# Where h tiles and down weights begin in SBUF, modulo 256 bytes, in a two-layer decoder kernel

## The chip, the cores and the metric

The kernel runs on one core of one Trainium2 chip. The metric is the device time of one execution in microseconds (us); lower is better.

## What is computed

Two layers (DEPTH = 2), each of three sub-layers: a SwiGLU feed-forward net (FFN), a token mixer with three kinds of attention heads, and a second FFN. The input has 256 tokens of width 1024, in float32. Cut to what matters here:

```python
def swiglu(h, w_gate, w_up, w_down):
    return (jax.nn.silu(h @ w_gate) * (h @ w_up)) @ w_down        # D_FF = 2816

for layer in range(DEPTH):
    g = norm_gains[layer]
    h = rmsnorm(x, g[0])
    x = x + 0.5 * rmsnorm(swiglu(h, w_ffn_gate[layer, 0], w_ffn_up[layer, 0], w_ffn_down[layer, 0]), g[1])
    h = rmsnorm(x, g[2])
    x = x + rmsnorm(token_mixer(h, w_in[layer], w_out[layer], ...), g[3])
    h = rmsnorm(x, g[4])
    x = x + 0.5 * rmsnorm(swiglu(h, w_ffn_gate[layer, 1], w_ffn_up[layer, 1], w_ffn_down[layer, 1]), g[5])
```

## The kernel before

**Split products.** Each float32 matrix is split into a high part (rounded to fp32r, by ScalarE) and a low part (the difference, by VectorE), and `mm3` (which calls `mm`, line 385) makes three matmuls of each product: high by high, high by low, low by high. Weights land in `raw` tiles by DMA and are split into a `ring` of ten tiles (ScalarE line 294, VectorE line 297).

**The FFN.** The 2816 hidden columns are handled as 11 pairs j of 256 (two chunks c of 128). In `gb(j)` the weights of gate and up are the stationary operand and the activations `xt` move, 256 columns a matmul, 96 matmuls a pair; line 605 is silu, line 607 the product, and lines 608 and 609 write its high and low parts to two `h` tiles of 512 columns: columns 256c + 128T belong to chunk c and token half T. In `down(j, T)` an h block of 128 columns is stationary and a row of 512 down weights moves, 12 matmuls: first the six of chunk 0, then the six of chunk 1 (each of two output halves n, three matmuls each). The first pair or two of an FFN go by `ga` and `hturn` in its place: there `xt` is stationary, and the product is transposed into the h tiles (lines 576, 582, 583).

**Order.** The loop runs `gb(j)`, `down(j - 1, 0)`, `down(j - 1, 1)`. For the pairs 6 to 10 (the set `skip`) `down(j, 1)` is put off; it comes at the end of the FFN by `LAST_ORDER = ((9, 0), (6, 1), (10, 0), (7, 1), (8, 1), (9, 1), (10, 1))`. So for the pairs 0 to 5 the two downs stand one behind the other, in each of the four FFNs: 24 such double downs. A list scheduler (`Program.run`) with a table of assumed durations decides the order on each engine.

**Places.** Tiles of the pools `xt`, `h2` and `ring` begin at a place: `AT_... = n` stands for 64 n bytes past a multiple of 256 bytes, by padding inside the tile (`PLACE` = 16 floats = 64 bytes, `Slots.take`). Blocks of 128 float32 columns are 512 bytes, so all blocks of a tile have their tile's place. `xt` has place 0. Gate, up and the other weights have place 1 (`AT_W`, `AT_X`), the h tiles place 1 (`AT_H`), the mixer's output weights and its own h tiles place 1 (`AT_O`), and the down weights have place 1 for chunk 0 and place 0 for chunk 1 (`AT_D = (1, 0)`). In this text the **distance** of a matmul is the place of the stationary block that is loaded for the next matmul less the place of the data that it streams itself, in bytes modulo 256. Before, chunk 0 of every down has distance 0, chunk 1 has 64, and `gb` has 64.

**Norms.** A norm takes the sum of squares with two ScalarE instructions (`sumsq`, line 428) whose squares go into `junk` tiles that nobody reads; then come GpSimd (lines 437, 438) and VectorE (457 for the residual, 476 for the normed rows), the transposes on TensorE (505), and the split into `xt` (508, 511). `junk` has two buffers, used in turn.

Of the kernel before, what the change touches and what calls it, by code (L numbers as in the profile page):

```python
# [8 lines left out]
F32 = mybir.dt.float32  # L9
F32R = mybir.dt.float32r  # L10
BF16 = mybir.dt.bfloat16
AF = mybir.ActivationFunctionType
OP = mybir.AluOpType
# [22 lines left out]
LAST_ORDER = ((9, 0), (6, 1), (10, 0), (7, 1), (8, 1), (9, 1), (10, 1))  # L36
# [31 lines left out]

BASE_PAD = 32
PLACE = 16  # L70
AT_W, AT_X, AT_O = 1, 1, 1
AT_H, AT_D = 1, (1, 0)


class Slots:
# [17 lines left out]
    def take(self, dtype, place=0):  # L93
        i = self.idle.pop(0)
        self.n += 1
        if self.places:
            u = self.whole(i, dtype)
            o = PLACE * ((place - i * (self.places - 1)) % 4)
            w = self.shape[1]
            t = [u[:, o + w * p:o + w * (p + 1)] for p in range(self.parts)]  # L100
        else:
            t = [self.pool.tile(self.shape, dtype, tag=f"{self.tag}{i}_{p}", name=f"{self.tag}{i}_{p}_{self.n}") for p in range(self.parts)]
        return i, (t[0] if self.parts == 1 else t)
# [17 lines left out]
class Program:  # L121
# [7 lines left out]
    def op(self, eng, dur, fn, after=(), bufs=(), spare=None, lag=None):  # L129
        o = Op()  # L130
        o.eng, o.dur, o.fn, o.after, o.bufs = eng, dur, fn, [a for a in after if a is not None], list(bufs)
        o.spare, o.lag, o.idx = spare or {}, lag, len(self.ops)
        for b in o.bufs:
            b.left += 1
        self.ops.append(o)
        return o
# [99 lines left out]
def act_us(n, psum, extra=0):  # L236
    return (0.05 if psum else 0.092) + 0.000833 * n + 0.093 * extra


def dve_us(n):  # L240
    return 0.068 + 0.00104 * n


def trunk(tc, x, norm_gains, w_gate, w_up, w_down, w_in, w_out, dlam, subln, consts, out):
    nc = tc.nc
    ctx = ExitStack()
    P1 = ctx.enter_context(tc.tile_pool(name="one", bufs=1))
# [4 lines left out]
    op = G.op  # L252
    PS = Slots(PSM, "ps", 8, [128, 512])
    P1.tile([128, BASE_PAD], F32, name="basepad")
    XTS = Slots(P1, "xt", 1, [128, KC * SEQ], 2, 1)
    H2 = Slots(P1, "h2", 12, [128, 512], 1, 4)
    RNG = Slots(P1, "ring", RING, [128, 1024], 2, 4)
    RAW = Slots(P1, "raw", NRAW, [128, 1024])
    ES = Slots(P1, "e", N_ES, [128, 512])
# [3 lines left out]
    SM = Slots(P1, "sm", 24, [128, 4])  # L263
    GPO = Slots(P1, "gpo", 1, [128, D])
    GPR = Slots(P1, "gpr", 1, [128, D])
    JK = Slots(P1, "junk", 2, [128, 512])
    QB = tuple(slice(32 * m, 32 * (m + 1)) for m in range(4))
    HB = (slice(0, 64), slice(64, 128))
    HALF = (slice(0, 512), slice(512, 1024))
# [1 line left out]
    def TS(T):  # L271
        return slice(128 * T, 128 * (T + 1))
# [42 lines left out]
    def half_row(w, r0, place):  # L315
        return half([(lambda t: t, w[r0:r0 + 128, :])], CUT_R, place)
# [44 lines left out]
    def warm():  # L361

        z, p = Buf(H2, BF16), Buf(PS)
        o = op("POOL", 0.2, lambda: nc.gpsimd.memset(z.t, 0.0), [], [z])

        def more(n, us, after):
            def pe():
                for _ in range(n):
                    mm(p.t, z.t[:, 0:128], z.t, True, True)

            op("PE", us, pe, [o, *after], [z, p])

        return more
# [10 lines left out]
    def mm(o, a, b, start=False, stop=False):  # L384
        nc.tensor.matmul(o, a, b, start=start, stop=stop, skip_group_check=True)  # L385
# [152 lines left out]
    def ffn(l, s, xt, na, turn1, g, final, nxt, pre):  # L538

        wg, wu, wd = w_gate[l, s], w_up[l, s], w_down[l, s]  # L540
        tiles = dict(pre)

        def tile_(kind, j):
            if (kind, j) not in tiles:
                if kind == "D":
                    tiles[kind, j] = [half_row(wd, 256 * j + 128 * c, AT_D[c]) for c in range(2)]
                else:
                    tiles[kind, j] = half_cols(wg if kind == "G" else wu, 256 * j, AT_X if j < na else AT_W)
            return tiles[kind, j]
# [3 lines left out]
        def hbuf(j):  # L553
            if j not in hb:
                hb[j] = (Buf(H2, F32R, AT_H), Buf(H2, F32R, AT_H))
            return hb[j]

        hdone = {}
        rows = {}
# [9 lines left out]
        def hturn(j, T):  # L569
            sg, m = rows[j, T]  # L570
            p = Buf(PS)
            bh, bl = hbuf(j)

            def pe():
                for c in range(2):
                    nc.tensor.transpose(p.t[:, 128 * c:128 * (c + 1)], sg.t[:, 256 + 128 * c:256 + 128 * (c + 1)], ident)  # L576

            def view(t):
                return t.rearrange("p (m t) -> p m t", m=2)

            o = op("PE", 0.22, pe, [m, o_ident], [p, sg])
            o1 = op("ACT", act_us(256, True), lambda: nc.scalar.activation(view(bh.t)[:, :, TS(T)], view(p.t[:, :256]), AF.Copy), [o], [p, bh])
            o2 = op("DVE", dve_us(256), lambda: nc.vector.tensor_tensor(view(bl.t)[:, :, TS(T)], view(p.t[:, :256]), view(bh.t)[:, :, TS(T)].bitcast(F32), OP.subtract),
                    [o1], [p, bh, bl])
            hdone[j, T] = [o2]

        def gb(j):
            sg = Buf(ES)
            a = None
            bh, bl = hbuf(j)  # L590
            for part in range(2):
                p = Buf(PS)
                hs = tile_("GU"[part], j)
                os = []
                for m in range(2):
                    for ks in steps(STEPS_G):
                        def pe(m=m, p=p, hs=hs, ks=ks):
                            for k in ks:
                                wh, wl = wk(hs, k)
                                c = TS(m)  # L600
                                mm3(p.t[:, 256 * m:256 * (m + 1)], wh[:, c], wl[:, c], xt.hi(k, slice(0, 256)), xt.lo(k, slice(0, 256)), m == 0 and k == 0, k == KC - 1)
                        use = [hs[i] for i in sorted({k // 4 for k in ks})]
                        os.append(op("PE", 0.327 * len(ks), pe, os[-1:] + sum(xt.done, []) + sum((h.ready for h in use), []), [p, xt.b] + [h.ring for h in use]))
                if part == 0:
                    a = op("ACT", act_us(512, True), lambda p=p: nc.scalar.activation(sg.t, p.t, AF.Silu), os[-1:], [p, sg])  # L605
                else:
                    m_ = op("DVE", dve_us(512), lambda p=p: nc.vector.tensor_tensor(sg.t, p.t, sg.t, OP.mult), os[-1:] + [a], [p, sg])  # L607
                    o1 = op("ACT", act_us(512, False), lambda: nc.scalar.activation(bh.t, sg.t, AF.Copy), [m_], [sg, bh])  # L608
                    o2 = op("DVE", dve_us(512), lambda: nc.vector.tensor_tensor(bl.t, sg.t, bh.t.bitcast(F32), OP.subtract), [o1], [sg, bh, bl])  # L609
                    hdone[j, 0] = hdone[j, 1] = [o2]  # L610

        acc = [Buf(PS) for _ in range(4)]
# [2 lines left out]
        def down(j, T):  # L615
            bh, bl = hbuf(j)
            last = j == NPAIR_FF - 1
            hs = tile_("D", j)
            for pieces in ([[(0, 0), (1, 0)], [(0, 1), (1, 1)]] if last else [[(0, 0), (0, 1)], [(1, 0), (1, 1)]]):
                cs = sorted({c for c, _ in pieces})  # L620
                ns = sorted({n for _, n in pieces})

                def pe(pieces=pieces):
                    for c, n in pieces:
                        o = slice(256 * c + 128 * T, 256 * c + 128 * (T + 1))
                        w = hs[c].ring.t
                        mm3(acc[2 * T + n].t, bh.t[:, o], bl.t[:, o], w[0][:, HALF[n]], w[1][:, HALF[n]], j == 0 and c == 0, last and c == 1)

                o = op("PE", 1.30, pe, hdone[j, T] + sum((done[2 * T + n] for n in range(2)), []) + sum((hs[c].ready for c in cs), []),
                       [acc[2 * T + n] for n in ns] + [bh, bl] + [hs[c].ring for c in cs])  # L630
                for n in (ns if last else range(2)):
                    done[2 * T + n] = [o]
# [13 lines left out]
        else:  # L646
# [1 line left out]
            hturn(0, 0)  # L648
            ga(0, 1)
            hturn(0, 1)  # L650
        skip = {j for j, T in LAST_ORDER if T == 1}
        for j in range(na, NPAIR_FF):
            gb(j)
            if j == NPAIR_FF - 1:
# [14 lines left out]
    def mixer(l, xt, turn1, g, nxt, o_cst, o_misc):  # L669
# [5 lines left out]
        def vstep(T, t):  # L675
            if vt[t] is None:
                vt[t] = half_v(wi, t)
            if t % 2 == 0:
                V[T, t // 2] = (Buf(PS), Buf(H2), [])
            p, v, os = V[T, t // 2]  # L680
            os.append(rows_op(p, 256 * (t % 2), xt, T, vt[t], t % 2 == 0))
            if t % 2 == 1:
                if t // 2:
                    o = op("ACT", act_us(512, True), lambda: nc.scalar.activation(v.t, p.t, AF.Copy), os, [p, v])
                else:
                    o = op("DVE", dve_us(512), lambda: nc.vector.tensor_copy(v.t, p.t), os, [p, v])
                vdone[T, t // 2] = o

        tab = [None]
# [247 lines left out]
        n = len(PAIRS)  # L937
# [162 lines left out]
```

## Time and profile before

| | |
|---|---|
| Three runs | 1002.55, 1003.51, 1003.85 us; median 1003.51 us |
| The profiled execution's own time | 1003.59 us |
| Its span, first to last instruction | 1001.8 us; so 1.8 us lie around it |
| TensorE matmuls (PE) busy | 986.3 us, 98% of the span |
| TensorE weight loads (PEld) busy | 909.8 us, 91% |
| VectorE (DVE), ScalarE (ACT), GpSimd (POOL) busy | 63%, 58%, 3% |
| Granted TensorE clock, mean | 0.999 of full speed |

Busy time of a matmul includes the part in which it overlaps the next, so a busy share near 100% says that TensorE has next to no idle time, not that its matmuls follow at the best rate. The rate is read from the distance between starts. The weight load of the next matmul starts within a few ns of the start of a matmul, so the starts of the PEld rows give it.

### The profile page before, as it was taken

The page shows a single profiled execution, that of the slowest core. Times are in us where ns is not written, and L with a number is a line of the kernel's source. Part 1 is how long each engine was busy: PE and PEld are TensorE (multiplying, and loading weights), DVE is VectorE, ACT ScalarE, POOL GpSimd, SP SyncE. Part 2 cuts the span into 40 slices and gives each one's busy share as a digit, 9 for nine tenths or more (in the row PEclk, how much of TensorE's full clock was granted, in tenths as well). Part 3 has the DMA queues.
Part 4 walks back from the last instruction along what each step waited for, and adds up shares of the span by engine and source line. Part 5 has one row for each costly group of instructions (what it writes and reads, how often), then busy time and mean ns, then how long its engine had stood idle before and what let it go on. Part 6 is the DMA issues. An engine that isn't in the chain of part 4 may idle for free.

```text
span 1001.8 us, 18113 instructions
## 1 busy us (share of the span) xinstructions
PE 986.3 (98%) x7144; PEld 909.8 (91%) x7144; DVE 632.5 (63%) x1123; ACT 582.8 (58%) x1133; POOL 34.3 (3%) x59
## 2 busy tenths in 40 slices
PE   8999999999999999999999999999999999999997
PEld 6999999898888999999899999999998789999995
DVE  6755544778898655444685554458799776545433
ACT  7654443769996545444665444446899765544441
POOL 1000000100001000000000000002000020000000
PEclk9999999999999999999999999999999999999999
DMA  8986664683335766665577666557732457666531
GB/s 265 335 271 192 189 184 147 196 252 106 109 116 177 248 185 190 197 188 151 171 227 233 194 191 199 152 169 237 204 106 85 155 161 233 188 195 187 167 105 43
DMA packets 157432, 182.86 MB, mean 183 GB/s; under 512 B 6049, under 2 KB 141473, under 8 KB 157218
## 3 DMA queue, kind: packets, MB, share of 16 engines
q1 hardware_dynamic: 157202, 181.43, 59.6%
q8 instruction: 56, 0.92, 0.4%
q14 instruction: 30, 0.25, 0.1%
q10 hardware_dynamic: 144, 0.26, 0.1%
HBM read 180.62 MB, written 1.05 MB: 181 GB/s over the span
## 4 chain that ended last, share of the span: by engine, by line
PE 87%; ACT 8%; DVE 2%; issue 1%; POOL 1%; DMA 0%; DVEq 0%; POOLq 0%; SPq 0%; ACTq 0%
PE ps L385 86%; ACT q L722 2%; ACT ring L294 1%; ACT q L738 1%; PE ps L505 1%; ACT e L789 1%; ACT junk L428 0%; DVE q L726 0%; ACT sn L867 0%; ACT sn L868 0%; DMA grow<-in_norm_gains 0%; ACT sn L866 0%; DVE q L742 0%; POOL sm L438 0%; PE ps L576 0%
## 5 line engine op out<-in xcount | busy, mean ns | idle before, releaser
L294 ACT ACTIVATE ring<-raw 128x512 fp32r<-128x512 f32 (+1 forms) x552 | 368.0, 706 | 319.8 <-issue 228.9
L297 DVE TENSOR_TENSOR ring<-raw,ring 128x512 fp32r<-128x512 f32 (+1 forms) x552 | 414.7, 788 | 198.4 <-ACT ring L294 192.5
L385 PE MATMUL ps<-xt,ring 128*128 128x256 f32 x4320 | 505.9, 277 | 0.0
L385 PEld LDWEIGHTS ps<-xt,ring 128*128 128x128 f32 x4320 | 499.9, 188 | 5.2 <-issue 1.7
L385 PE MATMUL ps<-ring,h 128*128 128x512 f32 x1248 | 299.7, 394 | 0.0
L385 PEld LDWEIGHTS ps<-ring,h 128*128 128x128 f32 x1248 | 229.6, 188 | 49.5 <-issue 0.3
L385 PE MATMUL ps<-ring,xt 128*128 128x256 f32 x1056 | 129.8, 281 | 1.5 <-DVE xt L511 1.5
L385 PEld LDWEIGHTS ps<-ring,xt 128*128 128x128 f32 x1056 | 126.5, 188 | 2.8 <-DVE xt L511 2.1
L607 DVE TENSOR_TENSOR e<-ps,e 128x512 f32<-128x512 f32 x37 | 25.6, 692 | 102.7 <-PE ps L385 102.7
L437 POOL TENSOR_SCALAR sm<-sm 128x1 f32<-128x1 f32 x24 | 15.8, 660 | 917.6 <-ACT junk L428 704.5
L608 ACT ACTIVATE h<-e 128x512 fp32r<-128x512 f32 x37 | 23.2, 626 | 21.3 <-DVE e L607 21.3
L453 DVE TENSOR_TENSOR e<-ps,gpo 128x512 f32<-128x512 f32 x24 | 16.4, 688 | 21.7 <-ACT junk L428 21.5
L428 ACT ACTIVATE junk<-ps 128x512 bf16<-128x512 f32 x24 | 14.3, 596 | 26.7 <-PE ps L385 25.6
L385 PE MATMUL ps<-q,q 128*128 128x256 f32 (+3 forms) x128 | 25.9, 295 | 3.1 <-DVE q L727 2.1
L738 ACT ACTIVATE q<-ps 64x256 fp32r<-64x256 f32 x72 | 27.1, 377 | 0.8
L385 PEld LDWEIGHTS ps<-q,q 128*128 128x128 f32 (+1 forms) x128 | 19.4, 187 | 8.5 <-issue 1.6
L605 ACT ACTIVATE e<-ps 128x512 f32<-128x512 f32 x37 | 21.9, 593 | 5.9 <-PE ps L385 5.8
L609 DVE TENSOR_TENSOR h<-e,h 128x512 fp32r<-128x512 f32 x37 | 25.3, 684 | 0.0
L789 ACT ACTIVATE e<-sn,sm 128x256 f32<-128x256 f32 (+1 forms) x56 | 24.7, 446 | 0.1
L722 ACT ACTIVATE q<-ps 32x256 fp32r<-32x256 f32 x64 | 24.0, 375 | 0.9
L742 DVE SCALAR_TENSOR_TENSOR q<-ps,q 64x256 fp32r<-64x256 f32 x48 | 20.2, 421 | 1.0
L508 ACT ACTIVATE xt<-ps 128x512 fp32r<-128x512 f32 x24 | 13.3, 591 | 11.5 <-PE ps L505 11.4
(86 smaller groups left out, 397.1 us busy)
## 6 DMA issues: line engine op xcount, KB each, us to landing
raw<-in_w_ffn_gate SPq DMA_DIRECT2D x88, 512.0 KB, 4.6
raw<-in_w_ffn_up SPq DMA_DIRECT2D x88, 512.0 KB, 4.7
raw<-in_w_ffn_down SPq DMA_DIRECT2D x88, 512.0 KB, 4.4
raw<-in_w_in SPq DMA_DIRECT2D x40, 512.0 KB, 5.3
raw<-in_w_out SPq DMA_DIRECT2D x16, 512.0 KB, 3.6
raw<-in_w_in SPq DMA_DIRECT2D x16, 256.0 KB, 4.2
gpo<-in_norm_gains SPq DMA_DIRECT2D x6, 512.0 KB, 5.8
gpr<-in_norm_gains SPq DMA_DIRECT2D x5, 512.0 KB, 5.1
```

The source lines that it names most:

```text
L294: nc.scalar.activation(h.ring.t[0][:, s], raw.t[:, s], AF.Copy)
L297: nc.vector.tensor_tensor(h.ring.t[1][:, s], raw.t[:, s], h.ring.t[0][:, s].bitcast(F32), OP.subtract)
L385: nc.tensor.matmul(o, a, b, start=start, stop=stop, skip_group_check=True)
L453: nc.vector.tensor_tensor(y.t, accs[i].t, gv(), OP.mult)
L605: a = op("ACT", act_us(512, True), lambda p=p: nc.scalar.activation(sg.t, p.t, AF.Silu), os[-1:], [p, sg])
L607: m_ = op("DVE", dve_us(512), lambda p=p: nc.vector.tensor_tensor(sg.t, p.t, sg.t, OP.mult), os[-1:] + [a], [p, sg])
L608: o1 = op("ACT", act_us(512, False), lambda: nc.scalar.activation(bh.t, sg.t, AF.Copy), [m_], [sg, bh])
L609: o2 = op("DVE", dve_us(512), lambda: nc.vector.tensor_tensor(bl.t, sg.t, bh.t.bitcast(F32), OP.subtract), [o1], [sg, bh, bl])
L722: nc.scalar.activation(b.t[QB[e], :], p.t[QB[m], :256], AF.Copy, scale=scale)
L738: nc.scalar.activation(bs[b].t[HB[b ^ e], :], p.t[HB[b], :256], AF.Copy, scale=scale)
L742: nc.vector.scalar_tensor_tensor(lo[b].t[HB[b ^ other], :], p.t[HB[b], :256], scale, bs[b].t[HB[b], :].bitcast(F32), OP.mult, OP.subtract)
L789: nc.scalar.activation(e.t[:, SEG[a]], sn.t[:, SEG[a]], AF.Exp, bias=mn.t[:, a:a + 1], scale=-1.0, accum_out=den.t[:, d0 + a:d0 + a + 1])
```

## The change

Down weights, h tiles and the mixer's output weights and h tiles all get place 0, the place of `xt`. The h tiles get 16 floats more, and from a cut on their columns lie 64 bytes further: for the pairs 6 to 10 all of chunk 1 (cut at 256), for the others the block of chunk 1 and token half 1 alone (cut at 384), which is the block that a double down reads last. Instructions that write h tiles are split at the cut, since no single run of columns crosses it. `junk` loses one of its two buffers.

```diff
-AT_W, AT_X, AT_O = 1, 1, 1
-AT_H, AT_D = 1, (1, 0)
+AT_W, AT_X, AT_O = 1, 1, 0
+AT_H, AT_D = 0, 0
...
-            o = PLACE * ((place - i * (self.places - 1)) % 4)
+            cols = self.parts * self.shape[1] + PLACE * (self.places - 1)
+            o = PLACE * ((place - i * (cols // PLACE)) % 4)
...
-    H2 = Slots(P1, "h2", 12, [128, 512], 1, 4)
+    H2 = Slots(P1, "h2", 12, [128, 512 + PLACE], 1, 4)
...
-    JK = Slots(P1, "junk", 2, [128, 512])
+    JK = Slots(P1, "junk", 1, [128, 512])
...
-                    tiles[kind, j] = [half_row(wd, 256 * j + 128 * c, AT_D[c]) for c in range(2)]
+                    tiles[kind, j] = [half_row(wd, 256 * j + 128 * c, AT_D) for c in range(2)]
...
+        skip = {j for j, T in LAST_ORDER if T == 1}
+
+        def hcut(j):
+
+            return 256 if j in skip else 384
+
+        def hcol(j, c, T):
+            o = 256 * c + 128 * T
+            o += PLACE if o >= hcut(j) else 0
+            return slice(o, o + 128)
+
+        def hparts(j):
+            n = hcut(j)
+            return (slice(0, n), slice(0, n)), (slice(n, 512), slice(n + PLACE, 512 + PLACE))
...
-            o1 = op("ACT", act_us(256, True), lambda: nc.scalar.activation(view(bh.t)[:, :, TS(T)], view(p.t[:, :256]), AF.Copy), [o], [p, bh])
...
+            o1 = op("ACT", 2 * act_us(128, True), fhi, [o], [p, bh])
+            o2 = op("DVE", 2 * dve_us(128), flo, [o1], [p, bh, bl])
...
-                    o1 = op("ACT", act_us(512, False), lambda: nc.scalar.activation(bh.t, sg.t, AF.Copy), [m_], [sg, bh])
-                    o2 = op("DVE", dve_us(512), lambda: nc.vector.tensor_tensor(bl.t, sg.t, bh.t.bitcast(F32), OP.subtract), [o1], [sg, bh, bl])
+
+                    def fhi():
+                        for f, t in hparts(j):
+                            nc.scalar.activation(bh.t[:, t], sg.t[:, f], AF.Copy)
+
+                    def flo():
+                        for f, t in hparts(j):
+                            nc.vector.tensor_tensor(bl.t[:, t], sg.t[:, f], bh.t[:, t].bitcast(F32), OP.subtract)
+
+                    o1 = op("ACT", act_us(256, False) * 2, fhi, [m_], [sg, bh])
+                    o2 = op("DVE", dve_us(256) * 2, flo, [o1], [sg, bh, bl])
...
-                        o = slice(256 * c + 128 * T, 256 * c + 128 * (T + 1))
+                        o = hcol(j, c, T)
```

On TensorE nothing moves. These are the rows of `down(1, 0)`, chunk 1, and `down(1, 1)`, chunk 0, in the first FFN, before (the h tiles with the lower number hold the high part, the others the low part):

```order
L385 MATMUL ps_0_16_508<-ring_16_503,h_4_532 128x512 x2
L385 MATMUL ps_0_16_508<-ring_16_503,h_5_546 128x512
L385 MATMUL ps_0_17_509<-ring_16_503,h_4_532 128x512 x2
L385 MATMUL ps_0_17_509<-ring_16_503,h_5_546 128x512
L385 MATMUL ps_0_18_538<-ring_15_474,h_4_532 128x512 x2
L385 MATMUL ps_0_18_538<-ring_15_474,h_5_546 128x512
L385 MATMUL ps_0_19_539<-ring_15_474,h_4_532 128x512 x2
L385 MATMUL ps_0_19_539<-ring_15_474,h_5_546 128x512
```

The changed kernel has the same eight rows in the same place, and so for all of TensorE; the names' last numbers and the line differ, and the addresses, which these rows don't print. On ScalarE, the instruction that writes the high part of h in `gb(3)` of the first FFN, with its neighbours, before and now:

```order
L294 ACTIVATE ring_28_838<-raw_0_28_726 128x1024
L294 ACTIVATE ring_29_875<-raw_0_29_737 128x512 x2
L608 ACTIVATE h_8_880<-e_0_5_835 128x512
L294 ACTIVATE ring_30_889<-raw_0_30_772 128x512 x2
...
L295 ACTIVATE ring_28_846<-raw_0_28_733 128x1024
L295 ACTIVATE ring_29_883<-raw_0_29_745 128x512 x2
L632 ACTIVATE h_8_888<-e_0_5_843 128x384
L632 ACTIVATE h_8_888<-e_0_5_843 128x128
L295 ACTIVATE ring_30_898<-raw_0_30_780 128x512 x2
```

One instruction has become two in its place; the same holds for VectorE behind it. In all, ScalarE and VectorE have 51 instructions more each (37 of `gb`, 14 of `hturn`). Last, ScalarE where the first layer's mixer ends: the squares of token half 0 of the mixer's output (from ps) and of the new x (from xs), before and now. The number right behind junk is the buffer:

```order
L428 ACTIVATE junk0_0_13_3708,sm22_0_47_3707<-ps6_0_91_3497 128x512
L428 ACTIVATE junk1_0_14_3718,sm22_0_47_3707<-ps2_0_92_3498 128x512
...
L428 ACTIVATE junk0_0_15_3745,sm23_0_49_3744<-xs_87 128x512
L428 ACTIVATE junk1_0_16_3748,sm23_0_49_3744<-xs_87 128x512
...
L429 ACTIVATE junk0_0_13_3732,sm22_0_47_3731<-ps6_0_91_3521 128x512
L429 ACTIVATE junk0_0_14_3742,sm22_0_47_3731<-ps2_0_92_3522 128x512
...
L429 ACTIVATE junk0_0_15_3769,sm23_0_49_3768<-xs_87 128x512
L429 ACTIVATE junk0_0_16_3772,sm23_0_49_3768<-xs_87 128x512
```

The order is the same, but each square now waits on ScalarE's own semaphore for the end of the square just before it, where it waited for the one before that. On SyncE and GpSimd nothing moves.

## Rows read from the trace of the kernel before

**Rows 1.** The page: span, TensorE's busy time, and the chain by engine.

```profile
span 1001.8 us, 18113 instructions
...
PE 986.3 (98%) x7144; PEld 909.8 (91%) x7144; DVE 632.5 (63%) x1123; ACT 582.8 (58%) x1133; POOL 34.3 (3%) x59
...
PE 87%; ACT 8%; DVE 2%; issue 1%; POOL 1%; DMA 0%; DVEq 0%; POOLq 0%; SPq 0%; ACTq 0%
```

**Rows 2.** The chain in order of time: one stretch of the first FFN.

```profile
29.23 164.53 PE ps L385 x1188
```

**Rows 3.** Timeline of weight loads, double down of pair 0 (start, us, what).

```profile
37.25 1.56 PEld L385 LDWEIGHTS ps<-ring,h 128*128 128x128 f32 x7
...
38.63 1.59 PEld L385 LDWEIGHTS ps<-ring,h 128*128 128x128 f32 x7
...
40.03 1.57 PEld L385 LDWEIGHTS ps<-ring,h 128*128 128x128 f32 x7
...
41.41 1.12 PEld L385 LDWEIGHTS ps<-ring,h 128*128 128x128 f32 x5
```

**Rows 4.** Timeline of weight loads: the first mixer's output product, places all 1.

```profile
308.51 8.35 PEld L385 LDWEIGHTS ps<-ring,h 128*128 128x128 f32 x37
```

**Rows 5.** Weight loads of gb: behind that down, 1.2 us later, and another gb.

```profile
42.81 0.88 PEld L385 LDWEIGHTS ps<-xt,ring 128*128 128x128 f32 x7
...
44.07 1.55 PEld L385 LDWEIGHTS ps<-xt,ring 128*128 128x128 f32 x13
...
26.02 1.60 PEld L385 LDWEIGHTS ps<-xt,ring 128*128 128x128 f32 x13
```

**Rows 6.** Weight loads of down(0, 0), chunk 0, second FFN, behind ga.

```profile
344.25 1.10 PEld L385 LDWEIGHTS ps<-ring,h 128*128 128x128 f32 x5
```

**Rows 7.** Timeline of ScalarE in the first mixer.

```profile
244.03 0.53 ACT L867 ACTIVATE sn<-sn 128x384 f32<-128x384 f32 x1
244.59 0.53 ACT L868 ACTIVATE sn<-sn 128x384 f32<-128x384 f32 x1
245.02 0.47 ACT L866 ACTIVATE sn<-ps 128x384 f32<-128x384 f32 x1
```

**Rows 8.** Timeline where the first mixer ends (idle time before, and what ended it).

```profile
309.39 0.60 ACT L428 ACTIVATE junk<-ps 128x512 bf16<-128x512 f32 x1 [3.25 <-PE ps L385]
309.88 0.19 ACT L428 ACTIVATION_READ_ACCUMULATOR junk<-ps 128x1 f32 x1
310.07 0.60 ACT L428 ACTIVATE junk<-ps 128x512 bf16<-128x512 f32 x1
...
313.33 0.61 ACT L428 ACTIVATE junk<-xs 128x512 bf16<-128x512 f32 x1
...
313.94 0.62 ACT L428 ACTIVATE junk<-xs 128x512 bf16<-128x512 f32 x1
...
320.22 8.52 PE L385 MATMUL ps<-ring,xt 128*128 128x256 f32 x70 [0.76 <-DVE xt L511]
```

**Rows 9.** The chain at the start, and two waits (us in total, times, longest).

```profile
11.47 1.32 ACT junk L428 x4
...
DVE pt L476 <- PE ps L385: 8.0, 2, 7.1
...
PE ps L385 <- DVE xt L511: 1.5, 2, 0.8
```

**Rows 10.** Timeline: h of the last pair, first FFN, and the downs behind it.

```profile
176.93 6.41 PE L385 MATMUL ps<-ring,h 128*128 128x512 f32 x27
177.20 0.69 DVE L607 TENSOR_TENSOR e<-ps,e 128x512 f32<-128x512 f32 x1 [3.14 <-PE ps L385]
...
180.08 0.68 DVE L609 TENSOR_TENSOR h<-e,h 128x512 fp32r<-128x512 f32 x1
```

**Rows 11.** Groups by form: writes of h of 512 and of 256 columns (busy, mean ns).

```profile
L609 DVE TENSOR_TENSOR h<-e,h 128x512 fp32r<-128x512 f32 x37 | 25.3, 684 | 0.0
...
L583 DVE TENSOR_TENSOR h<-ps,h 128x256 fp32r<-128x256 f32 x14 | 5.8, 417 | 0.0
```

More of the change, by code (lines that the diff above doesn't have):

```diff
@@ L363, in warm @@
         z, p = Buf(H2, BF16), Buf(PS)
-        o = op("POOL", 0.2, lambda: nc.gpsimd.memset(z.t, 0.0), [], [z])
+        o = op("POOL", 0.2, lambda: nc.gpsimd.memset(z.t[:, 0:512], 0.0), [], [z])
         def more(n, us, after):
@@ L368, in pe @@
                 for _ in range(n):
-                    mm(p.t, z.t[:, 0:128], z.t, True, True)
+                    mm(p.t, z.t[:, 0:128], z.t[:, 0:512], True, True)
             op("PE", us, pe, [o, *after], [z, p])
@@ L576, in pe @@
                     nc.tensor.transpose(p.t[:, 128 * c:128 * (c + 1)], sg.t[:, 256 + 128 * c:256 + 128 * (c + 1)], ident)
-            def view(t):
-                return t.rearrange("p (m t) -> p m t", m=2)
+            def fhi():
+                for m in range(2):
+                    nc.scalar.activation(bh.t[:, hcol(j, m, T)], p.t[:, TS(m)], AF.Copy)
+            def flo():
+                for m in range(2):
+                    c = hcol(j, m, T)
+                    nc.vector.tensor_tensor(bl.t[:, c], p.t[:, TS(m)], bh.t[:, c].bitcast(F32), OP.subtract)
             o = op("PE", 0.22, pe, [m, o_ident], [p, sg])
-            o1 = op("ACT", act_us(256, True), lambda: nc.scalar.activation(view(bh.t)[:, :, TS(T)], view(p.t[:, :256]), AF.Copy), [o], [p, bh])
-            o2 = op("DVE", dve_us(256), lambda: nc.vector.tensor_tensor(view(bl.t)[:, :, TS(T)], view(p.t[:, :256]), view(bh.t)[:, :, TS(T)].bitcast(F32), OP.subtract),
-                    [o1], [p, bh, bl])
+            o1 = op("ACT", 2 * act_us(128, True), fhi, [o], [p, bh])
+            o2 = op("DVE", 2 * dve_us(128), flo, [o1], [p, bh, bl])
             hdone[j, T] = [o2]
@@ L607, in gb, with fhi, flo @@
                     m_ = op("DVE", dve_us(512), lambda p=p: nc.vector.tensor_tensor(sg.t, p.t, sg.t, OP.mult), os[-1:] + [a], [p, sg])
-                    o1 = op("ACT", act_us(512, False), lambda: nc.scalar.activation(bh.t, sg.t, AF.Copy), [m_], [sg, bh])
-                    o2 = op("DVE", dve_us(512), lambda: nc.vector.tensor_tensor(bl.t, sg.t, bh.t.bitcast(F32), OP.subtract), [o1], [sg, bh, bl])
+                    def fhi():
+                        for f, t in hparts(j):
+                            nc.scalar.activation(bh.t[:, t], sg.t[:, f], AF.Copy)
+                    def flo():
+                        for f, t in hparts(j):
+                            nc.vector.tensor_tensor(bl.t[:, t], sg.t[:, f], bh.t[:, t].bitcast(F32), OP.subtract)
+                    o1 = op("ACT", act_us(256, False) * 2, fhi, [m_], [sg, bh])
+                    o2 = op("DVE", dve_us(256) * 2, flo, [o1], [sg, bh, bl])
                     hdone[j, 0] = hdone[j, 1] = [o2]
@@ L650, in ffn @@
             hturn(0, 1)
-        skip = {j for j, T in LAST_ORDER if T == 1}
         for j in range(na, NPAIR_FF):
@@ L683, in vstep @@
                 if t // 2:
-                    o = op("ACT", act_us(512, True), lambda: nc.scalar.activation(v.t, p.t, AF.Copy), os, [p, v])
+                    o = op("ACT", act_us(512, True), lambda: nc.scalar.activation(v.t[:, 0:512], p.t, AF.Copy), os, [p, v])
                 else:
-                    o = op("DVE", dve_us(512), lambda: nc.vector.tensor_copy(v.t, p.t), os, [p, v])
+                    o = op("DVE", dve_us(512), lambda: nc.vector.tensor_copy(v.t[:, 0:512], p.t), os, [p, v])
                 vdone[T, t // 2] = o
```

## The prediction

> **What bounds the kernel now.** I first read the page: TensorE is busy for 98% of the span, and 87% of the chain that ended last is TensorE [rows 1]. The chain in order of time then shows how solid that is: one unbroken stretch of 164.53 us and 1188 matmuls in the first FFN [rows 2], in which TensorE waits for no other engine. So in the FFNs the only things that count are the number of matmuls, which the change leaves alone, and the time from the start of one to the start of the next. I read that from the timeline of weight loads, one row for each six matmuls of a double down [rows 3]. The starts are 37.25, 38.63, 40.03, 41.41 us, and the next gb begins at 42.81 [rows 5]. So the first piece (T = 0, c = 0, distance 0) takes 1.38 us, c = 1 (distance 64) 1.40, then for T = 1 again 1.38 and 1.40. Matmuls of one shape, with the same operands waiting in SBUF, differ in pace, and the place is what differs.
>
> How good can distance 0 get? The mixer's output product has distance 0 throughout, and once it runs undisturbed it makes 36 steps in 8.35 - 0.19 = 8.16 us, 0.2267 us each [rows 4] (0.19 us is the last load's own length): 1.36 us for six. Chunk 1's 1.40 us is 0.2333 us each. The 1.38 us of the c = 0 pieces lies between them: it holds a few steps of settling after the distance has changed.
>
> **The change, part by part.** *Double downs.* Of the four pieces of a double down, the change gives the second distance 0 as well, so that the first three have one distance and only the last keeps 64. The second goes from 1.40 to 1.36 us (0.04 won). The third no longer comes behind a change of distance and goes from 1.38 to 1.36 (0.02 won). The fourth stays at 1.40: it had distance 64 and has it still, behind a piece of distance 0 in both kernels. That is 0.06 us each. There are 24 double downs; in three of them (pair 0 of the FFNs that start with two pairs by ga) transposes break the row in the middle, and I count half, 0.03. Sum: 21 x 0.06 + 3 x 0.03 = 1.35 us.
>
> *Single downs.* The pairs 6 to 10 gain nothing. Their chunk 0 had distance 0 and has it, their chunk 1 had 64 and has it (h moved on by 64 bytes over down weights at 0, where it was h at 64 over weights at 0). All seven downs of `LAST_ORDER` are of these pairs. Likewise the mixer's output product: both operands move from place 1 to 0, the distance stays 0. So the change touches 24 x 12 of the 1056 matmuls of the downs, a quarter of them.
>
> *The way in.* The last matmul of a gb streams xt (place 0) while the first h block is loaded, which moves from place 1 to 0: distance 64 before, 0 now. The trace of before has that entry only behind ga: there the four steps behind the first take 1.10 - 0.19 = 0.91 us, 0.2275 each [rows 6], so it settles rather sooner than the 1.38 us piece does. There are 40 such entries (10 loop downs in each of 4 FFNs). Bounds: at best the piece takes 1.36 (40 x 0.02 = 0.8 us won; from unrounded starts it is nearer 0.6), at worst the settling costs 0.01 more (0.4 us lost). I take 0, since the nearest row (rows 6) lies between and its way in is another engine state.
>
> *The way out.* The gb behind a down starts with 0.115 us a matmul [rows 5] (0.88 - 0.19 over six) and goes at 0.1133 from then on (1.55 - 0.19 over twelve). Since the last piece has distance 64 and its steady 0.2333 in both kernels, I let this stand.
>
> *Split h writes.* 51 more instructions on ScalarE and as many on VectorE. A 512-column subtraction takes 0.684 us, a 256-column one 0.417 [rows 11], so a split costs some 0.15 us of VectorE, and I take the same for ScalarE. Behind them wait the ring copies in the queues, which have 42% and 37% of the span idle [rows 1], and the down that reads h. In the loop that comes a whole gb later (96 x 0.1133 = 10.9 us [rows 5]). The tightest place is pair 10: its h is ready at 180.08 + 0.68 = 180.76 us, and the downs begin at 176.93 with `down(9, 0)` and `down(6, 1)`, 24 matmuls or 5.56 us, so it is read at 182.49 [rows 10]. The slack of 1.7 us covers 0.3. Cost 0; without that cover it would be 0.3 us in each FFN, 1.2 in all.
>
> *One junk buffer.* A square must now wait for the one just before it. What a ScalarE instruction pays for waiting on its predecessor can be read where it does so already: line 868 needs the result of 867 and starts 0.56 us after it, while the next independent instruction starts 0.43 us after 868 [rows 7]. So 0.13 us for each pair of squares that stand back to back. Of the 24 pairs most are hidden: those of FFN ends behind the remaining downs or the next ga, the first of all behind the gain rows on TensorE, for which VectorE waits 7.1 us [rows 9]. On the path lie three: token half 1 at the start (the chain runs 1.32 us through its squares [rows 9]), and the new x of token half 0 where a mixer ends, twice: those squares start 0.61 us apart, and at the end of that chain TensorE sits idle 0.76 us for VectorE's xt [rows 8, 9]. The pair from PSUM just before starts at 310.07, which is when the read behind the first square ends (309.88 + 0.19), so there only some 0.03 us is left to pay, twice [rows 8]. Sum: 3 x 0.13 + 2 x 0.03 = 0.45 us lost.
>
> *Sum.* 1.35 - 0.45 = 0.90 us won. The profiled execution took 1003.59 us (span 1001.8 and 1.8 around it), so 1002.7; the median of the three runs lies 0.08 lower, so **1002.6 us**. What a measurement of this kernel can tell from no change is about 0.2%, 2.0 us; 0.9 us is within it.
>
> **A rule that speaks against it.** In [rows 3] the place changes the pace by 0.0067 us a matmul, 3%. The Trainium skill, page "TensorE: Matmul & The Clock Gate", section "Step-by-step: what each phase is for", says that TensorE reads weights and moving data through two independent SBUF ports, so that loading the next weights takes nothing from the running matmul. By that rule the double downs would win nothing and the sum would be the junk wait alone. The trace disagrees with it by that 3%, which no wait of another engine explains.
>
> **Rivals.** *Place is not the cause* (by that page's rule, but as a mechanism here: chunk 1 is slower for another reason, say because its six matmuls come second). Then 1.35 falls away and 1002.6 + 1.35 = 1003.95 us. Against it: in [rows 4] later pieces of a row don't slow down.
>
> *It never settles.* If the new way in leaves the first piece in a pace of 0.230, and distance 0 keeps it through all three, a double down wins 0.02 at most (1.38 three times for 1.38, 1.40, 1.38), so 0.5 us in all, and time ends near 1003.5. Against it: the mixer's product settles, from several ways in, within about a dozen matmuls.
>
> *It settles at once, and more is hidden.* With all 40 entries at their best the sum is 1.35 + 0.6 - 0.45 = 1.5 us won, 1002.0; without the junk waits too, 1001.56. That is the one that could pass the 2.0 us.
>
> *The way out falls into the slow pace.* Gb has two paces at one distance: 0.1133 us in most stretches, and 0.1175 (1.60 - 0.19 over twelve) at 26.02 us, also with weights at place 1 and xt at 0, right behind ga [rows 5]. What came before decides. If down now left TensorE so that a gb stays in the slow one, each of 36 gbs would lose 96 x 0.0042 = 0.40 us, 14.5 us in all: 1017. Three gbs are enough to turn the gain into a loss, seven or eight to make it slower by over 0.2%. Against it: the last six matmuls have the same distance, at the same places (0 and 64), as before.
>
> **How the numbers follow.** Chances: the forecast 0.70; place not the cause 0.07; never settles 0.06; settles at once 0.12; slow way out 0.05. Faster by over 0.2%: half of "at once" and an eighth of the forecast, 0.15. Slower by over 0.2%: the slow way out and some of the spread above the "no cause" case, 0.07. Within 0.2%: 0.78. The range takes in 1003.95 with some scatter of single runs (the three runs span 1.3 us) and reaches down past 1001.56: 1001.2 to 1004.2. It leaves out the slow way out and the tails.
>
> **What would show it.** Right: in a timeline of weight loads behind the first double down, starts 1.38 or less, 1.36, 1.36 and 1.40 us apart; no change in pairs 6 to 10; gb still at 0.1133; squares of the new x some 0.74 us apart, where they were 0.61, and the idle 0.76 us longer by as much. Wrong: a second piece of 1.40, a gb at 0.1175, or a wait of TensorE inside an FFN for the split h writes.

## The result and the profile after

The changed kernel takes **1018.31 us** (median of 1018.05, 1018.15, 1018.47, 1018.69), against 1003.57 us for the kernel before, measured beside it (1002.55 to 1003.85): a ratio of 1.0149, 95% interval 1.0137 to 1.0161. It is slower by some 15 us, far outside the range. The profiled execution took 1018.05 us, with a granted TensorE clock of 0.999 of full speed as before, so the clock has no part in it.

From the page of the changed kernel: span, TensorE, and two groups of matmuls, with `xt` and with `h` (busy us, mean ns of one).

```profile
span 1016.3 us, 18224 instructions
...
PE 1001.1 (99%) x7144; PEld 925.3 (91%) x7144; DVE 635.6 (63%) x1174; ACT 588.1 (58%) x1184; POOL 31.0 (3%) x59
...
L386 PE MATMUL ps<-xt,ring 128*128 128x256 f32 x4320 | 520.2, 281 | 0.0
...
L386 PE MATMUL ps<-ring,h 128*128 128x512 f32 x1248 | 298.9, 394 | 0.0
```

The same two groups of the page of the kernel before, which the rows above the prediction don't hold:

```profile
L385 PE MATMUL ps<-xt,ring 128*128 128x256 f32 x4320 | 505.9, 277 | 0.0
...
L385 PE MATMUL ps<-ring,h 128*128 128x512 f32 x1248 | 299.7, 394 | 0.0
```

The loss is TensorE's own busy time (986.3 in [rows 1], 1001.1 now), and nearly all of that is in matmuls that the change does not touch: those that stream `xt`, `gb` above all, are 14.3 us longer at the same count, while the downs, which it does touch, are 0.8 us shorter. The chain in order of time says the same: the stretch of [rows 2] is as unbroken as it was, and 3.5 us longer for the same 1188 matmuls.

```profile
29.25 168.06 PE ps L386 x1188
```

The timeline of weight loads at the first double down and the gb behind it (start, us, what), as in [rows 3, 5]:

```profile
37.27 1.57 PEld L386 LDWEIGHTS ps<-ring,h 128*128 128x128 f32 x7
...
38.66 1.55 PEld L386 LDWEIGHTS ps<-ring,h 128*128 128x128 f32 x7
...
40.02 1.55 PEld L386 LDWEIGHTS ps<-ring,h 128*128 128x128 f32 x7
...
41.38 1.12 PEld L386 LDWEIGHTS ps<-ring,h 128*128 128x128 f32 x5
...
42.77 0.90 PEld L386 LDWEIGHTS ps<-xt,ring 128*128 128x128 f32 x7
...
44.07 1.60 PEld L386 LDWEIGHTS ps<-xt,ring 128*128 128x128 f32 x13
```

The pieces take 1.39, 1.36, 1.36 and 1.39 us, as forecast to 0.01. But the gb starts at (0.90 - 0.19) / 6 = 0.118 us a matmul and stays at (1.60 - 0.19) / 12 = 0.1175, where before it ran at 0.1133. That is the slow pace of [rows 5]. Summed from starts in the two traces, the 36 gbs that stand behind a down took 392.08 us before and 407.04 now, 0.416 us more each and 14.96 us in all. Every one of the 36 is slow.

Rows round to 0.01 us, and what follows needs a finer grain. So here are the intervals from one start to the next, in ns, from the same trace records: the last seven before the first matmul of a gb, then the first six of the gb.

```
                                      last of the down              | gb
before, first gb behind a down        227 233 233 234 233 233 234   | 121 116 114 114 113 113
before, same of the second FFN        231 231 236 231 236 231 236   | 118 113 114 113 113 114
after, first gb behind a down         226 236 231 236 230 236 231   | 118 118 117 118 118 118
```

The mean of the last six before the bar is 233.3, 233.5 and 233.3. But there are two kinds of such rows, steady and alternating. Before, an alternating row stood ahead of one gb in each FFN but the first, and ended on 236; now it stands ahead of every gb and ends on 230 or 231. Below, a last interval of 231 or less is called short and one of 232 or more long.

### The profile page after: what moved, and what is told of

The parts are those of the page before. It is cut to its first block, busy times and chain, and to the rows that moved or that the text cites. A ratio compares the mean times of both kernels' runs of the same rounds, so it can differ in the third digit from the quotient of the medians.

```text
span 1016.3 us, 18224 instructions
## 1 busy us (share of the span) xinstructions
PE 1001.1 (99%) x7144; PEld 925.3 (91%) x7144; DVE 635.6 (63%) x1174; ACT 588.1 (58%) x1184; POOL 31.0 (3%) x59
## 3 DMA queue, kind: packets, MB, share of 16 engines
HBM read 180.62 MB, written 1.05 MB: 179 GB/s over the span
## 4 chain that ended last, share of the span: by engine, by line
PE 88%; ACT 7%; DVE 2%; issue 2%; POOL 0%; DMA 0%; DVEq 0%; POOLq 0%; SPq 0%; ACTq 0%
PE ps L386 86%; ACT q L751 2%; ACT ring L295 1%; ACT q L767 1%; PE ps L506 1%; ACT e L818 1%; ACT junk L429 0%; DVE q L755 0%; ACT sn L896 0%; ACT sn L897 0%; ACT sn L895 0%; DMA grow<-in_norm_gains 0%; POOL sm L439 0%; DVE q L771 0%; PE ps L592 0%
## 5 line engine op out<-in xcount | busy, mean ns | idle before, releaser
L386 PE MATMUL ps<-xt,ring 128*128 128x256 f32 x4320 | 520.2, 281 | 0.0
L386 PEld LDWEIGHTS ps<-xt,ring 128*128 128x128 f32 x4320 | 513.9, 189 | 5.1 <-issue 1.7
L438 POOL TENSOR_SCALAR sm<-sm 128x1 f32<-128x1 f32 x24 | 13.7, 572 | 935.1 <-ACT junk L429 935.1
L632 ACT ACTIVATE h<-e 128x256 fp32r<-128x256 f32 (+1 forms) x74 | 26.7, 409 | 22.6 <-DVE e L628 22.6
L429 ACT ACTIVATE junk<-ps 128x512 bf16<-128x512 f32 x24 | 14.3, 596 | 27.1 <-PE ps L386 25.9
L636 DVE TENSOR_TENSOR h<-e,h 128x256 fp32r<-128x256 f32 (+1 forms) x74 | 27.9, 420 | 0.0
```

The costliest lines, as they stand in the source:

```text
L632: nc.scalar.activation(bh.t[:, t], sg.t[:, f], AF.Copy)
L636: nc.vector.tensor_tensor(bl.t[:, t], sg.t[:, f], bh.t[:, t].bitcast(F32), OP.subtract)
```

## The experiments

In all of them the gb's own operands keep their places (`xt` 0, weights 1, distance 64) unless said. One theory stood at the start, **rhythm**: the way in which the last piece of a down runs sets the pace of the gb behind it, and that way depends on which operand makes the step to distance 64 (the down weights before, the h block now). Its rivals were the split writes, the long row at distance 0 that runs at a settled 0.2267 us ahead of the last piece, and the places of gb themselves.

**Writes only.** The changed kernel with the places of before:

```diff
-AT_W, AT_X, AT_O = 1, 1, 0
-AT_H, AT_D = 0, 0
+AT_W, AT_X, AT_O = 1, 1, 1
+AT_H, AT_D = 1, (1, 0)
...
-            o += PLACE if o >= hcut(j) else 0
```

> The kernel before with the places of before, but with the split writes of h and the one junk buffer of the change. Theory 'rhythm' (the places set how the last piece of a down runs, and that sets the pace of the gb behind it): the places are those of before, so gb stays at 0.1133 us a matmul and the time is 1003.6 + 0.45 for the junk waits = 1004.0 us (1003.2 to 1004.8). Rival 'writes' (the split writes or the junk wait slow TensorE): gb at 0.1177 and about 1018 us.

Measured: 1003.84 us against 1003.37, ratio 1.0006 (0.9997 to 1.0015); every gb fast. The split writes and the one junk buffer are not the cause. The 0.47 us is near the 0.45 forecast for junk, but the interval also takes in no difference.

**A break ahead of each gb.** The changed kernel, with

```diff
+                            if part == 0 and m == 0 and ks[0] == 0:
+                                for _ in range(2):
+                                    nc.tensor.transpose(p.t[:, 0:128], ident, ident)
```

> The changed kernel with two idle transposes of the identity on TensorE ahead of each gb, whose result is overwritten. Theory 'rhythm': the pace is inherited from the matmuls just before, so the transposes cut it and gb runs at 0.1133 again: 36 x 96 x 0.0042 = 14.5 us back, less 37 x 0.25 us for the transposes and the settling behind them = 9.2, so about 1013 us. Rival 'the places or the writes themselves set the pace of gb, whatever runs before': gb stays at 0.1177 and the time is 1018.3 + 9 = 1027 us.

Measured: 1018.73 us, ratio 1.0157 (1.0142 to 1.0172), near neither. The timeline of weight loads in three gbs that follow each other, of this kernel:

```profile
44.76 1.60 PEld L386 LDWEIGHTS ps<-xt,ring 128*128 128x128 f32 x13
...
61.76 1.55 PEld L386 LDWEIGHTS ps<-xt,ring 128*128 128x128 f32 x13
...
78.42 1.60 PEld L386 LDWEIGHTS ps<-xt,ring 128*128 128x128 f32 x13
```

Slow, fast, slow: 18 of the 36 gbs are fast and 18 slow. The transposes don't cut anything off: ahead of the slow ones the down's last interval is 230 or 231 ns, ahead of the fast ones 232 to 237. In the first FFN a down behind a slow gb ends long and one behind a fast gb ends short, so they take turns. A break costs some 0.22 us in this trace (108 and 28 ns for the transposes, and a first step of gb of 201 ns in place of 118). So 18 x 0.416 = 7.5 us come back and 37 x 0.22 = 8.1 us go: 0.6 us over the changed kernel, where 0.4 was measured.

**h steps at each chunk.** One line of the changed kernel, `return 256 if j in skip else 384`, becomes `return 256`.

> The changed kernel with the h shift at column 256 in every pair, so that the four pieces of a double down have the distances 0, 64, 0, 64 of the kernel before, but reached by a step of the h block and not of the down weights; the last piece has the very places of before. Theory 'rhythm': the last piece still begins by a step of h, so it runs 236 and 231 ns in turn and gb is slow in all pairs: 1018.3 + 24 x 0.06 = about 1019.7 us. Rival 'long run' (the three pieces at one distance, settled at 0.2267, put gb into the slow pace): no such run is left, gb at 0.1133, about 1004 us.

Measured: 1019.74 us, ratio 1.0166 (1.0149 to 1.0183); all 36 gbs slow. The first of them, in the timeline of weight loads:

```profile
44.14 1.60 PEld L386 LDWEIGHTS ps<-xt,ring 128*128 128x128 f32 x13
```

So the long settled row is not needed: with the four distances of the kernel before, and the last piece at the very places of before, the gb is slow when h made the step.

**The down weights step.** Distances 0, 0, 0, 64, with the step made by the down weights:

```diff
-AT_W, AT_X, AT_O = 1, 1, 0
-AT_H, AT_D = 0, 0
+AT_W, AT_X, AT_O = 1, 1, 1
+AT_H, AT_D = 0, (1, 0)
...
-            o = 256 * c + 128 * T
-            o += PLACE if o >= hcut(j) else 0
+            o = 272 + 128 * T if c == 0 else 144 * T
+            if j in skip:
+                o = PLACE + 256 * c + 128 * T
```

This was run twice. In the first the block (c = 1, T = 1) stood at column 272, over one of chunk 0, so some products use other data; the places and the matmuls are the same. The diff shows the second.

> Distances 0, 0, 0, 64 as in the changed kernel, split writes and one junk buffer too, but the last step is made by the down weights, as in the kernel before: chunk 0 of the down weights at 64 and chunk 1 at 0, and of h only the block (c = 1, T = 0) at 0, all else at 64; the skip pairs are as before. Theory 'rhythm': the last six run steadily at 0.2333, gb at 0.1133, and the 1.35 us of the double downs are won: 1003.6 - 1.35 + 0.45 = 1002.7 us. Rival 'long run': gb behind the double downs (24 less those of pair 0 broken by transposes) slow, 24 x 0.4 = 9.7 us, so about 1012 us. Rival 'steps of h of any kind': the weights of T = 0 now step by h from chunk 0 to 1 together with the down weights; if that counts, gb is slow too.

> The kernel in which the down weights make the last step, with the block of h at its right column and all matmuls: 1003.1 us as before the mending (1002.7 to 1003.5), gb fast everywhere, since the pieces ahead of it end on 236 behind the pairs 0 to 5 and run steadily at 0.2333 behind the others.

Measured: 1003.06 us, ratio 0.9998 (0.9989 to 1.0008), and 1003.19 us, 0.9996 (0.9988 to 1.0005). All gbs are fast. But the theory as stated is wrong: the last piece alternates here too, and the gb is fast all the same. What differs is where the alternation stands at the end.

```
after                                 226 236 231 236 230 236 231   | 118 118 117 118 118 118
the down weights step                 231 232 236 230 236 231 236   | 118 114 113 113 114 113
```

If h steps, the last matmul of the piece before already loads a block at distance 64 (that is the 226), so seven matmuls ahead of the gb have it; if the down weights step, six have. So I formed a second theory, **parity**: behind a step from a settled row long and short intervals take turns (226, 236, 231, 236 if h steps), and a gb that is entered behind a short one locks into the slow pace, behind a long one into the fast.

**One matmul fewer, in both kernels.** It leaves out a product of high h by low weight in the last piece of each down ahead of a gb, in the changed kernel and in the one whose down weights step:

```diff
+                        if (c, n) == (1, 1) and j < 9 and T == (0 if j in skip else 1):
+                            mm(acc[2 * T + n].t, bh.t[:, o], w[0][:, HALF[n]])
+                            mm(acc[2 * T + n].t, bl.t[:, o], w[0][:, HALF[n]])
+                            continue
```

> The changed kernel, with one matmul left out (a low product, h high by weight low, of the last half) in the last piece of each down ahead of a gb: five in place of six. Theory 'parity' (behind the step to distance 64 the starts alternate 236, 231; a gb that is entered behind a 231 locks into 0.1177, behind a 236 into 0.1133): the piece ends on 236, gb is fast: 1018.3 - 36 x 0.2333 - 36 x 0.41 = 1018.3 - 8.4 - 14.8 = 995.1 us. Rival 'the kind of step sets the pace' (h steps: slow): 1018.3 - 8.4 = 1009.9 us.

> The kernel in which the down weights make the last step (whose gbs were fast, behind a piece that ran 231, 236, 231, 236, 231, 235), with the h block that it had put at a wrong column mended, and with one matmul left out of the last piece ahead of each gb. Theory 'parity': the piece now ends on 231 and gb is slow: 1003.1 - 8.4 + 14.8 = 1009.5 us. Rival 'the kind of step sets the pace': gb stays fast, 1003.1 - 8.4 = 994.7 us.

Measured: 994.19 us, ratio 0.9911 (0.9896 to 0.9926), for the first; 1004.88 us, 1.0019 (1.0010 to 1.0029), for the second. In the timeline of weight loads the first has its gb fast:

```profile
43.68 1.55 PEld L386 LDWEIGHTS ps<-xt,ring 128*128 128x128 f32 x13
```

The second has it slow behind the double downs (first row) and fast behind the pairs 6 to 8 (second row):

```profile
43.80 1.60 PEld L386 LDWEIGHTS ps<-xt,ring 128*128 128x128 f32 x13
...
140.65 1.55 PEld L386 LDWEIGHTS ps<-xt,ring 128*128 128x128 f32 x13
```

One matmul taken away repairs the one kernel and spoils the other. In the second the pairs 6 to 8 run steadily at 233, with nothing to turn over; that I had overlooked. With 24 slow gbs in place of 36 the expected time is 994.7 + 24 x 0.416 = 1004.7 us, and 1004.88 was measured.

**No step at all, with six and with five matmuls.** The changed kernel without the shift of h (the line with `hcut` in `hcol` and the shift in `hparts` taken out), and the same with one matmul fewer as above:

> The changed kernel without the 64-byte shift of h: distance 0 through the whole of every down, and only the last matmul of a down, which loads the first block of gb, has distance 64. From the changed kernel it wins 24 + 44 last pieces at 1.36 in place of 1.40 us = 2.7 us, so 1015.6 us if gb stays slow and 1000.8 if it is fast. Theory 'parity', counted from the step: one matmul at distance 64 ahead of gb, an odd number as the seven of the changed kernel, so slow: 1015.6 us. If only the kind of step or the alternation itself matters, it is open.

> The kernel without the shift of h, with the same matmul left out as before (five in the last piece). Theory 'parity' counts the matmuls from the step to distance 64, not those of the piece: the steady row at 0.2267 has no long and short ones, one matmul at distance 64 stays one, gb stays slow: 1014.7 - 8.4 = 1006.3 us. Rival 'the number of matmuls in the piece or the program as such': gb fast, 1006.3 - 14.8 = 991.5 us.

Measured: 1014.69 us, ratio 1.0111 (1.0096 to 1.0126), and 1007.20 us, 1.0035 (1.0021 to 1.0049). All gbs are slow in both, behind intervals of 227, 226, 227 and a last one of 225 or 226; the first gb without the shift:

```profile
43.76 1.60 PEld L386 LDWEIGHTS ps<-xt,ring 128*128 128x128 f32 x13
```

Here only the last matmul of a down, which loads the first block of gb, has distance 64. Taking a matmul away ahead of it leaves the pace of gb as it was, so the number of matmuls in the piece is not what counts; a count of the matmuls since the step, one in both kernels, fits.

**Only the low block shifted.** The high part of the last h block stays in place (and is written by one instruction again), so within the piece only the two matmuls that load the low block have distance 64. The last matmul, which loads the first block of gb, has it too, so the last two ahead of gb do:

```diff
-                        mm3(acc[2 * T + n].t, bh.t[:, o], bl.t[:, o], w[0][:, HALF[n]], w[1][:, HALF[n]], j == 0 and c == 0, last and c == 1)
+                        mm3(acc[2 * T + n].t, bh.t[:, TS(2 * c + T)], bl.t[:, o], w[0][:, HALF[n]], w[1][:, HALF[n]], j == 0 and c == 0, last and c == 1)
```

> The changed kernel, in which only the low part of the last h block lies 64 bytes further, its high part does not. So the last piece runs at distance 0 but where a low block is loaded, and leaves with two matmuls at distance 64 (the one that loads the last low block, and the one that loads the first block of gb). Theory 'parity' (from a settled row the starts behind the step go 226, 236, 231, 236: odd numbers end short and gb is slow, even ones end long and gb is fast): two, so about 226, 236 and gb at 0.1133: the kernel without the shift, 1014.7 - 14.8 + 0.5 for the unsettled steps = 1000.4 us. Rival 'a step made by h leaves gb slow': 1015.2 us.

Measured: 1001.28 us, ratio **0.9977** (0.9968 to 0.9986): faster than both kernels, with every product computed. Its last piece and the gb, in the timeline of weight loads:

```profile
41.20 1.10 PEld L386 LDWEIGHTS ps<-ring,h 128*128 128x128 f32 x5
...
43.84 1.55 PEld L386 LDWEIGHTS ps<-xt,ring 128*128 128x128 f32 x13
```

The last five intervals are 226 236 228 229 236, then in gb 119 113 113 114: the end is long, and all 36 gbs are fast. The first low block has broken the settled row before the last step comes, so this run bears out the long end more than the count.

**Other places for the other weights.** All at place 0 (without the shift of h), and, on top of the kernel with the low block, gate and up of the `ga` pairs and V at place 3 (`AT_X = 3`):

> As the kernel without the shift, and all other weights (gate, up, the mixer's) begin at the activations' place too: distance 0 in every ring matmul. If distance 0 settles for 256 columns as it does for 512 (0.2267, so 0.1133), nothing alternates and no gb is slow: from the kernel before, 1003.4 + 0.45 - 24 x 0.12 - 44 x 0.06 for the downs - 1056 x 0.0043 for the products of ga and V that run at 0.118 = about 993.8 us. Rival: 256 columns at distance 0 have a slow pace of their own, 0.1177 for gb: 993.8 + 14.8 = 1008.6 us.

> As the kernel in which only the low block is shifted, and the weights of ga and of V begin at 192 in place of 64: there the weights are what is streamed and xt what is loaded, so their distance becomes 0 - 192 = 64 (mod 256), that of gb, where it was 192 with 0.118 us a matmul in all of the trace. If distance 64 is what allows 0.1133, whichever operand is at which place, ga and V take up to 1056 x 0.0045 = 4.7 us less: 1000.4 - 4.7 = 995.7 us. If only the sign or the operand counts, no change, 1000.4.

Measured: 1025.54 us, ratio 1.0221 (1.0206 to 1.0237), for all at 0; 999.60 us, **0.9959** (0.9946 to 0.9971), for the other. The first lies above what either side had forecast. Of that kernel, the weight loads of a gb in the timeline, and the group of matmuls that stream `xt` on the page:

```profile
44.62 1.63 PEld L386 LDWEIGHTS ps<-xt,ring 128*128 128x128 f32 x13
```

```profile
L386 PE MATMUL ps<-xt,ring 128*128 128x256 f32 x4320 | 531.2, 283 | 0.0
```

(1.63 - 0.19) / 12 = 0.1200 us: at distance 0, the best one for 512 columns, 256 columns run slower than in either pace at 64. The group is 531.2 - 505.9 = 25.3 us above that of before. In the second the group that streams weights past `xt` shrank, but by less than forecast; its row on the page, without the place 3 and with it:

```profile
L386 PE MATMUL ps<-ring,xt 128*128 128x256 f32 x1056 | 129.8, 282 | 1.5 <-DVE xt L512 1.5
```

```profile
L386 PE MATMUL ps<-ring,xt 128*128 128x256 f32 x1056 | 126.8, 280 | 1.7 <-DVE xt L512 1.7
```

3.0 us of the 4.7 are there: part of these rows take the fast pace (median 113 ns) and part the slow. By starts, 615 of 1036 steps within these rows are at 112 to 114 ns. But without the place 3, at distance 192, 115 of 1036 are so too, where the changed kernel has none; so distance 64 is not what allows the fast pace. It is the fastest kernel of the study that computes every product; its median is 1.7 us below that of the kernel with the low block.

**All gbs together.** In the twelve traces in which a down runs straight into a gb at distance 64 (all but the one with transposes and the one with all at 0; before and after are among them), 36 gbs each, 432 in all, the last interval before the gb tells its pace without an exception: the 72 gbs behind 225 or 226 and the 96 behind 230 or 231 are slow, the 264 behind 233 to 236 fast.

A row that no down stands ahead of goes the same way: the first 96 matmuls for queries and keys in each mixer, also 256 columns at distance 64, which stand behind the row for the values V. In all traces but the one with all at 0, 26 such rows, the 16 behind a last interval of 115 ns are slow, the 10 behind 117 to 122 fast. In the trace of before both are slow and in that of the changed kernel both are fast, though the change leaves the places of both groups alone; in the kernel with the low block one is fast and one slow. So places alone don't fix the pace there either. Little time hangs on it, since TensorE soon waits for other engines.

## Why the prediction was wrong

**The step that failed is "The way out"**: "Since the last piece has distance 64 and its steady 0.2333 in both kernels, I let this stand." The 0.2333 held as a mean of six; "steady" did not. It now alternates between 231 and 236, enters gb behind a 231, and the slow pace of gb that I had read in [rows 5] holds for all of its 96 matmuls. 36 x 0.416 = 15.0 us, which the fourth rival had at 14.5 us and 1017 us, with a chance of 0.05. My argument against it, that the last six matmuls have the same distance and places as before, is refuted by the run in which h steps at each chunk: same distances, same places in the last piece, and slow. What precedes the piece counts too; what differs there is the matmul just ahead of it, which loads its first h block and had distance 0 before and has 64 now. The trace of before already held the evidence: three of its gbs stand behind an alternating row. They happen to end on 236, and I had read the pieces only as sums of six.

**Double downs: right, a little too large.** From starts, the 21 unbroken ones took 5.555 us each before and 5.507 now: second piece 1.400 to 1.360, third 1.380 to 1.359, fourth 1.400 in both, as forecast; the first went from 1.375 to 1.387. That is 0.048 in place of 0.06, 1.0 us in place of 1.26. The three broken ones gained their 0.03. **Place not the cause** falls: the second piece would have stayed at 1.40. In the experiments 256 columns ran at 0.1133, 0.1178 and 0.1200 us with the same matmul, by place and by what ran before. The rule of the Trainium skill, page "TensorE: Matmul & The Clock Gate", section "Step-by-step: what each phase is for", is that weights and moving data come through two independent SBUF read ports, so that loading the next weights takes no read bandwidth from the running matmul. The runs disagree with what the prediction drew from it, that places would not matter; what in the reading of the operands makes them matter, no run shows.

**Way in: taken as 0, cost 0.4 us**, the bound that I had given. Of the 40 entries that I counted, 37 stand behind a gb; the other three stand behind ga, as before. By starts, each of the 37 first pieces takes 0.012 us more: 0.25 us in the 21 double downs (it is in their 0.048 already) and 0.19 in the 16 others. Behind those first pieces, the downs of `LAST_ORDER`, which I had said gain nothing, lose 0.04 us in each FFN, 0.15 in all.

**Split h writes: 0, as forecast.** At pair 10 the downs begin at 180.43 and h is ready at 183.57 + 0.76 = 184.33 us, in this timeline; 24 matmuls later (5.6 us) is 186.0. The cover is 1.7 us, as before [rows 10].

```profile
180.43 6.90 PE L386 MATMUL ps<-ring,h 128*128 128x512 f32 x29
...
181.59 0.70 ACT L632 ACTIVATE h<-e 128x256 fp32r<-128x256 f32 x2
...
183.57 0.76 DVE L636 TENSOR_TENSOR h<-e,h 128x256 fp32r<-128x256 f32 x2
```

**Junk: right.** In the chain at the start the four instructions took 1.32 us [rows 9] and now 0.72 + 0.02 + 0.72, 0.14 more. Where the first mixer ends, the timeline has the squares of the new x 0.74 us apart, as forecast, and of PSUM's pair 0.74 for 0.68:

```profile
312.87 0.60 ACT L429 ACTIVATE junk<-ps 128x512 bf16<-128x512 f32 x1 [3.23 <-PE ps L386]
...
313.61 0.60 ACT L429 ACTIVATE junk<-ps 128x512 bf16<-128x512 f32 x1
...
316.80 0.61 ACT L429 ACTIVATE junk<-xs 128x512 bf16<-128x512 f32 x1
...
317.54 0.63 ACT L429 ACTIVATE junk<-xs 128x512 bf16<-128x512 f32 x1
...
323.84 2.39 PE L386 MATMUL ps<-ring,xt 128*128 128x256 f32 x18 [0.75 <-DVE xt L512]
```

The idle time itself did not grow (0.75 for 0.76 in [rows 8]), where I had looked for the price; the row of transposes ahead of it is stretched instead (from its start to the matmuls behind it 1.05 us now, 0.93 before). From the first square to TensorE's restart it is 10.97 us where it was 10.83, 0.14 for a forecast 0.16.

**The sum.** By TensorE's starts in the two traces: 14.96 for gb, -1.02 and -0.10 for the double downs, 0.19 and 0.15 for the other downs, 0.36 for junk (0.14 at the start, 0.12 and 0.10 where the mixers end, for a forecast 0.45), and -0.13 because the row of gains that TensorE waits for first landed earlier. That makes 14.41 us; the profiled executions differ by 14.46. Single stretches of the mixers moved by up to 0.2 us, in both directions, and nearly cancel.

**What stays open.** Why a short last interval leads to one pace and a long one to the other, and why there are two, no run shows. The last interval may itself be a sign of the state and not its cause; what is shown is that the number of matmuls since the step turns it over in both directions.

## What to carry to other kernels

Where back-to-back matmuls have a pace that depends on places, a change of places in one group can set the pace of the next group, so its price must be looked for in matmuls that the change doesn't touch. "Same distance, same mean pace at the handover" is no argument that the next group runs as before: look at single starts, not at sums of six, and search the trace of before for both states of the row behind. And a place that is best for one width need not be for another: try each group by itself.

## What the runs showed of the hardware that I had not expected

- Matmuls of 256 columns at one distance (64) and the same two places (0 and 64, modulo 256) hold either 113.3 or 117.8 ns a matmul for 96 in a row, from the first few on; nothing in the row itself turns it over.
- Rows of 512 columns at distance 64 hold 233.3 ns steadily or alternate 231 and 236 with the same mean, according to what stood before.
- Two transposes between a down and a gb (0.2 us on TensorE) don't reset this: the 36 gbs behind them are slow behind a down that ended on 230 or 231 and fast behind one on 232 to 237.
- At distance 0, 512 columns settle at 226.7 ns, but 256 columns at 120.0.
